# Two mixers of a transformer trunk: a written letter order in place of an emission order from estimates, with TensorE held to it

## The chip, the core and the metric

The kernel runs on one core of a Trainium2 chip. A core has five engines with a queue each: TensorE (PE in the profile; PEld is its weight load), VectorE (DVE), ScalarE (ACT), GpSimd (POOL) and SyncE (SP), which issues the transfers. The metric is the time of one execution in microseconds.

## The reference

A trunk of four residual layers on 512 tokens of width 1024, in FP32. Every layer is half a SwiGLU feed-forward, a mixer, and half a feed-forward again. The mixer of the first layer pair (A) is RWKV-7 time mixing on 12 heads beside a 4-head attention over 256 memory rows; that of the second (B) is dilated sliding-window attention beside the same memory attention. `DEPTH = 2` gives one mixer of each kind, and four feed-forwards.

```python
def step(state, inp):                       # RWKV-7, one token of one head
    r_t, w_t, k_t, v_t, kk_t, a_t = inp
    sa = jnp.einsum('bhvk,bhk->bhv', state, -kk_t)
    state = (state * w_t[:, :, None, :] + sa[..., None] * (kk_t * a_t)[:, :, None, :]
             + v_t[..., None] * k_t[:, :, None, :])
    return state, jnp.einsum('bhvk,bhk->bhv', state, r_t)

logits = jnp.einsum('bshd,bmhd->bhsm', q, k).astype(jnp.float32) / math.sqrt(HEAD_DIM)
probs = jax.nn.softmax(logits, axis=-1)     # memory attention, both mixers
```

## The kernel before

**Products.** All tiles hold features on partitions and the 512 tokens along the free side. A wide FP32 product is made of three matmuls per 128-deep chunk, with both factors split into a high and a low part (`uh`, `ul` against `whi`, `wlo`); those of the mixers' projections show as `mm<-uh,whi`, `mm<-ul,whi`, `mm<-uh,wlo`, and those of the output projections of mixer B as `mm<-kvh,whi` and so on.

**Strands.** The feed-forwards run one after the other. Each mixer is written as a set of generators, the strands, which yield between their steps. In A (`mixer_a`, L654): `finish`, `scan(0)`, `scan(1)`, `prepare`, `memory(0)`, `memory(1)`, `projections`, `first_pass`. In B (`mixer_b`, L1108): `memory`, `dilated(0)`, `dilated(1)`, `settle`, `projections`, `first_pass`. For each of the six head pairs of A, `projections` makes k, r and v; `prepare` makes the decays `E`, the tiles `AR`, `beta`, `kappa`; `scan` (function `rwkv_solve`) multiplies `AR` with `beta` and with `kappa`, masks the first product into `mb` (VectorE), makes `tx` and `TT` from it (GpSimd), transposes in 32x32 blocks (VectorE), and inverts a triangular matrix level by level with small products `sc<-tx,mb` and `sc<-TT,tx`; `finish` carries the state `H` from chunk to chunk (`py<-pt,H` and `py<-H,G`, then ScalarE writes the next `H`) and reads out `y`. `memory` makes logits (`sc<-tmp,memkv`), softmax (VectorE maximum `mx`, ScalarE exponential into `krv` in A or `mpr` in B, VectorE scale), and transposes on TensorE (`sc<-cst,krv`, `sc<-cst,mpr`). `dilated` does the like with `sc<-kh,qn`, `prob`, `dmx`, and `sc<-cst,prob`.

**What sets the order.** `weave` (L312, called at L764 and L1255) picks the next strand to step. Every instruction goes through a helper (`call` in `Engine`, L294, which is therefore the line of all rows below) that adds an estimated cost to a clock per engine in `Meter` (L230). A strand that yields `WAIT` is not stepped until the estimated TensorE clock has reached the estimated end of what it waits for; of those ready the first in the list is taken. `until(test)` holds a strand until other strands have got so far. This gives the order of emission. On top of it the framework's scheduler reorders the instructions of every engine, TensorE too, by its own cost model.

```python
def until(test):
    if not test():
        yield test
```

Of the kernel before, what the change touches and what calls it, by code (L numbers as in the profile page):

```python
# [223 lines left out]
        return r  # L224


WAIT, FREE = "wait", "free"


# [79 lines left out]
            setattr(self, n, Engine(self.meter, n, getattr(nc, n)))  # L309


def weave(meter, strands):  # L312


    live = [[0.0, None, s] for s in strands]
    for x in live:
        x[0] = meter.clock["tensor"]
    while live:
        now = meter.clock["tensor"]
        for x in live:  # L320
            if x[1] and x[1]():
                x[0], x[1] = max(x[0], now), None
        able = [x for x in live if not x[1]]
        assert able, "all strands wait"
        cur = ([x for x in able if x[0] <= now] or [min(able, key=lambda x: x[0])])[0]
        meter.end = max(now, cur[0])
        try:
            said = next(cur[2])
        except StopIteration:
            live.remove(cur)  # L330
            continue
        if callable(said):
            cur[1] = said
        elif said is WAIT:
            cur[0] = meter.end


def until(test):
    if not test():
        yield test  # L340


def run(gen):
    for _ in gen:
        pass


class Net:
# [305 lines left out]
    def mixer_a(self, xin, u, kv, mid, nexts, dst, after):  # L654
        nc, tc = self.nc, self.tc
        w = self.ap["wa_in"]
        with ExitStack() as ctx:
            pool = ctx.enter_context(tc.tile_pool(name="mixa", bufs=1, reuse_waits="tile"))
            pp = ctx.enter_context(tc.tile_pool(name="psa", bufs=2, space=PSUM, reuse_waits="tile"))

            def bank(tag, shape=(P, T)):
                return self.take(pp, list(shape), F32, tag, BANKS[tag])
# [35 lines left out]
            def projections():  # L698
                ps = [bank("mm"), bank("mm")]
                for i, step in enumerate(self.dense([(ps[0], w[0]), (ps[1], w[1])], u.parts, 2)):  # L700
                    if i == 4:
                        rr.append(u.rstd(bank("sc")))
                    yield step
                shifted(ps[0], 0, self.lo)
                nc.scalar.activation(self.lo[:HD], self.lo[:HD], AF.Tanh)
                shifted(ps[1], 1, self.gl)
                nc.scalar.activation(self.gl, self.gl, AF.Tanh, scale=0.5)
                nc.vector.tensor_scalar(self.gl, self.gl, 0.5, 0.5, op0=ALU.mult, op1=ALU.add)
                for j in range(NPAIR):
                    yield from until(lambda: j < 2 or self.made[j - 2])  # L710

                    self.lora[j] = pool.tile([P, 2, P], F32, tag="lora", bufs=3, name=self.nm("lora"))
                    nc.sync.dma_start(self.lora[j][:, 0], self.ap["lo_up"][:, j * P:(j + 1) * P])
                    nc.sync.dma_start(self.lora[j][:, 1], self.ap["g_up"][:, j * P:(j + 1) * P])
                    tiles = []
                    for i in range(3):
                        ps = bank("mm")
                        yield from self.dense([(ps, w[2 + 3 * j + i])], u.parts)
                        t = self.big("krv", 6)
                        shifted(ps, 2 + 3 * j + i, t)  # L720
                        tiles.append(t)
                    self.krv[j] = tiles
                for i in range(2):
                    ps = bank("mm")
                    yield from self.dense([(ps, w[20 + i])], u.parts)
                    nc.vector.tensor_tensor(om[i], ps, rr[0], op=ALU.mult)
                    q.append(om[i])

            def memory(j):
                yield from until(lambda: len(q) > j)  # L730
                r = yield from self.head_rms(q[j], T, self.tmp, bank, keep=self.query_roots[:, j])
                yield from until(lambda: self.made[NPAIR - 1])
                yield from self.memory_attention(j, q[j], r, kv, pool, bank, om[j])

            def spare():
                return tuple(self.xp.tile([P, T], F32R, tag=t, bufs=KD, name=self.nm(t)) for t in ("uh", "ul"))

            def prepare():
                for j in range(NPAIR):
                    yield from until(lambda: self.krv[j] and (j < 2 or len(ys) > j - 2))  # L740
                    yield from self.rwkv_prepare(j)

            def scan(par):
                for j in range(par, NPAIR, 2):
                    yield from until(lambda: self.made[j])
                    yield from self.rwkv_solve(j)

            def finish():
                for j in range(NPAIR):
                    yield from until(lambda: self.made[j])  # L750
                    y = self.big("y", 8)
                    yield from self.rwkv_finish(j, y)
                    ys.append(y)

            def first_pass():
                yield from until(lambda: len(ys) >= NPAIR - 1)
                parts = [spare() for _ in ys[:NPAIR - 1]]
                for p, y in zip(parts, ys):
                    self.split_into(*p, y)
                    yield WAIT  # L760
                yield from self.project_out(xin, parts, 0, "wa_out", bank, [], mid)

            self.busy_vector = True
            weave(self.meter, [finish(), scan(0), scan(1), prepare(), memory(0), memory(1), projections(), first_pass()])  # L764
            pairs = [self.big("AR", 2, (P, 2, T), F32R) for _ in range(2)]
            parts = [(t[:, 0], t[:, 1]) for t in pairs] + [tuple(self.big("krv", 6, dtype=F32R) for _ in range(2))]
            for p, y in zip(parts, (ys[5], om[0], om[1])):
# [340 lines left out]
    def mixer_b(self, xin, u, rkv, ukv, kv, bdram, mid, nexts, dst, after):  # L1108
        nc, tc = self.nc, self.tc
        wq, wkv = self.ap["wb_q"], self.ap["w_kv"]  # L1110
        with ExitStack() as ctx:
            pool = ctx.enter_context(tc.tile_pool(name="mixb", bufs=1, reuse_waits="tile"))
            pp = ctx.enter_context(tc.tile_pool(name="psb", bufs=2, space=PSUM, reuse_waits="tile"))

# [30 lines left out]
            def projections():  # L1145
                for s in range(2):
                    for kind in "qkv":
                        for m in (s, 2 + s, 4 + s):
                            yield from until(lambda: len(later) < 3)
                            yield from project(kind, m)  # L1150
                    if s == 0:
                        for m in (6, 7):
                            yield from project("q", m)

            def settle():
                n = 0
                while n < 20:
                    yield from until(lambda: later)
                    kind, m, t = later.pop(0)
                    n += 1  # L1160
                    if kind == "v":
                        yield WAIT
                        ps = self.turned(lambda b: t[:, b * P:(b + 1) * P])
                        nc.scalar.activation(vt[:, :, m * P:(m + 1) * P], ps, AF.Copy)
                        yield WAIT
                    elif kind == "k":
                        yield from self.head_norm(kh[:, m], t, self.gain(2), self.tmp, bank, T)
                    else:
                        rq[m] = yield from self.head_rms(t, T, self.tmp, bank, keep=self.query_roots[:, m])
                    done.add((kind, m))  # L1170
# [66 lines left out]
            def memory():  # L1237
                for j in range(2):
                    yield from until(lambda: ("q", 6 + j) in done)
                    yield from self.memory_attention(j, q[6 + j], rq[6 + j], kv, pool, bank, om[2 + j])  # L1240
                    remembered.append(j)
# [8 lines left out]
            def first_pass():  # L1250
                yield from until(lambda: len(remembered) == 2 and len(finished) >= 5)
                yield from self.project_out(xin, operands([2, 3]), 0, "wb_out", bank, [], mid)

            self.busy_vector = True
            weave(self.meter, [memory(), dilated(0), dilated(1), settle(), projections(), first_pass()])  # L1255
            run(self.project_out(mid, operands([0, 1]), 2, "wb_out", bank, nexts, dst, ("py", "mm", "sc", "sc"), 3, q))
            self.busy_vector = False
            after()
# [84 lines left out]
```

## Time and profile before

| | us |
|---|---|
| time, median of 3 runs | 2103.12 (2101.11 to 2108.2) |
| profiled execution | 2113.38 |
| its span | 2111.6 |
| mean granted TensorE clock | 0.989 |
| TensorE busy | 2061.6 (98% of the span), 14594 instructions |
| VectorE, ScalarE, GpSimd busy | 867.3, 817.3, 590.7 |

The mixers take the stretches from 386 to 773 us (A) and from about 1541 to 1741 us (B) of the span; what lies outside them is the four feed-forwards. Times within the span are given from its start.

### The profile page before, as it was taken

How to read it: one execution, taken by the hardware profiler on the slowest of the kernel's cores; microseconds unless marked ns; L12 is line 12 of the kernel's file. 1: busy time of each engine (PE TensorE's matmuls, PEld its weight loads, DVE VectorE, ACT ScalarE, POOL GpSimd, SP SyncE). 2: the span in 40 equal slices, each digit the busy share in tenths (PEclk: the TensorE clock that was granted, in tenths of full speed). 3: DMA queues.
4: the chain of work that ended last, by engine and by line, in shares of the span. 5: the costliest groups of instructions: out<-in, count | busy, mean ns of one | idle time of the engine just before them, and what ended most of it. 6: DMA issues, size and time to landing. Idle time of an engine off the chain costs nothing.

```text
span 2111.6 us, 35927 instructions
## 1 busy us (share of the span) xinstructions
PE 2061.6 (98%) x14594; PEld 1670.4 (79%) x14594; DVE 867.3 (41%) x1294; ACT 817.3 (39%) x1418; POOL 590.7 (28%) x513
## 2 busy tenths in 40 slices
PE   8999999989999899999999999999999999999999
PEld 6888888867777677788888888888787768888887
DVE  6333333454555555333343533333326266333322
ACT  6333333423334554333433433333336455333321
POOL 2222222553432152222222222222232224222221
PEclk9999999999999999999999999999999999999999
DMA  5333344411100173353344433334531144333342
GB/s 195 97 95 100 90 127 133 122 47 35 40 29 25 35 244 116 116 166 95 110 138 127 146 99 96 98 103 127 154 95 48 38 156 162 99 96 99 92 138 80
DMA packets 130645, 222.13 MB, mean 105 GB/s; under 512 B 14232, under 2 KB 31824, under 8 KB 130480
## 3 DMA queue, kind: packets, MB, share of 16 engines
q1 hardware_dynamic: 130480, 219.85, 34.0%
q8 instruction: 114, 1.87, 0.4%
q14 instruction: 51, 0.42, 0.1%
HBM read 202.90 MB, written 21.61 MB: 106 GB/s over the span
## 4 chain that ended last, share of the span: by engine, by line
PE 65%; DVE 1%; ACT 0%; issue 0%; POOL 0%; ACTq 0%; POOLq 0%; DVEq 0%
PE fps L294 52%; PE mm L294 7%; PE sc L294 5%; PE py L294 1%; DVE prob L294 0%; DVE x L294 0%; DVE mpr L294 0%; ACT krv L294 0%; DVE mx L294 0%; POOL wlo L294 0%; DVE dmx L294 0%; ACT mpr L294 0%; DVE tmp L294 0%; ACT L294 0%; DVE krv L294 0%
## 5 line engine op out<-in xcount | busy, mean ns | idle before, releaser
L294 POOL TENSOR_TENSOR wlo<-raw,whi 128x512 fp32r<-128x512 f32 (+3 forms) x404 | 496.7, 1231 | 1414.0 <-ACT whi L294 1398.1
L294 ACT ACTIVATE whi<-raw 128x512 fp32r<-128x512 f32 (+3 forms) x684 | 415.7, 610 | 924.4 <-PE fps L294 782.0
L294 PE MATMUL fps<-uh,whi 128*128 128x512 f32 x1408 | 551.8, 392 | 8.2 <-ACT whi L294 8.2
L294 PE MATMUL fps<-uh,wlo 128*128 128x512 f32 x1408 | 550.5, 391 | 0.6 <-POOL wlo L294 0.6
L294 PE MATMUL fps<-ul,whi 128*128 128x512 f32 x1408 | 549.1, 390 | 0.0
L294 DVE TENSOR_TENSOR wlo<-raw,whi 128x512 fp32r<-128x512 f32 x280 | 201.7, 721 | 343.7 <-ACT whi L294 338.7
L294 PEld LDWEIGHTS fps<-uh,whi 128*128 128x128 f32 x1408 | 264.9, 188 | 68.7 <-ACT whi L294 12.9
L294 PEld LDWEIGHTS fps<-uh,wlo 128*128 128x128 f32 x1408 | 265.2, 188 | 58.6 <-POOL wlo L294 3.1
L294 PEld LDWEIGHTS fps<-ul,whi 128*128 128x128 f32 x1408 | 265.0, 188 | 55.8 <-issue 0.7
L294 PE MATMUL fps<-hh,whi 128*128 128x512 f32 x704 | 273.9, 389 | 0.0
L294 PE MATMUL fps<-hl,whi 128*128 128x512 f32 x704 | 273.9, 389 | 0.0
L294 PE MATMUL fps<-hh,wlo 128*128 128x512 f32 x704 | 273.9, 389 | 0.0
L294 DVE TENSOR_TENSOR gs<-fps,rstd 128x512 f32<-128x512 f32 x88 | 60.5, 690 | 321.6 <-PE fps L294 321.6
L294 PEld LDWEIGHTS fps<-hh,whi 128*128 128x128 f32 x704 | 132.2, 188 | 27.7
L294 PEld LDWEIGHTS fps<-hh,wlo 128*128 128x128 f32 x704 | 132.2, 188 | 27.3
L294 PEld LDWEIGHTS fps<-hl,whi 128*128 128x128 f32 x704 | 132.2, 188 | 27.3
L294 PE MATMUL mm<-uh,whi 128*128 128x512 f32 x280 | 124.6, 445 | 0.4 <-DVE p L294 0.2
L294 PE MATMUL mm<-ul,whi 128*128 128x512 f32 x280 | 114.5, 409 | 0.1
L294 PE MATMUL mm<-uh,wlo 128*128 128x512 f32 x280 | 113.6, 406 | 0.0
L294 DVE TENSOR_TENSOR hm<-fps,gs 128x512 f32<-128x512 f32 x88 | 60.6, 691 | 121.9 <-PE fps L294 115.7
L294 DVE TENSOR_TENSOR hl<-hm,hh 128x512 fp32r<-128x512 f32 x88 | 77.2, 880 | 50.7 <-ACT hh L294 50.7
L294 PEld LDWEIGHTS mm<-uh,whi 128*128 128x128 f32 x280 | 54.1, 193 | 16.2 <-issue 4.4
(260 smaller groups left out, 2049.6 us busy)
## 6 DMA issues: line engine op xcount, KB each, us to landing
raw<-w SPq DMA_DIRECT2D x512, 256.0 KB, 2.7
raw<-wa_in SPq DMA_DIRECT2D x44, 256.0 KB, 2.8
xd<-x SPq DMA_DIRECT2D x40, 256.0 KB, 2.7
tmp<-xd SPq DMA_DIRECT2D x32, 256.0 KB, 4.2
xin<-xd SPq DMA_DIRECT2D x32, 256.0 KB, 4.3
raw<-w_kv SPq DMA_DIRECT2D x24, 256.0 KB, 2.7
raw<-w SPq DMA_DIRECT2D x32, 128.0 KB, 2.4
raw<-wmem SPq DMA_DIRECT2D x16, 256.0 KB, 2.6
```

The lines of the kernel that those rows point to most:

```text
L294: r = f(*args, **kw)
```

## The change

`weave` gets a string for each mixer. Each letter stands for one step of one strand (`a` is the first in the list, `b` the second, and so on). A letter whose strand still waits in `until` is owed and taken as soon as its test holds. `until` now always yields once. The `Meter`'s estimates are no longer asked. In both mixers a manual schedule is set for TensorE, so that its instructions keep the order in which they are emitted. The other engines are still ordered by the framework's scheduler, now from another order of emission.

```diff
+ORDER_A = (
+    "abcdeaefhhhhhhggggggggfgggggggggggggggggggggggggggggggggggggdddgddggggddddddggdgggggddbbbbbbbggggggb"
...
+ORDER_B = (
+    "ccccabdedfeeeeeeeeeeeeeeeeeeeddddeeddddeeeeeeeeeddddeebbeeebbeeeedaadeedeeddeeeeeddeeeedddeeeeeeedde"
...
-def weave(meter, strands):
...
-        cur = ([x for x in able if x[0] <= now] or [min(able, key=lambda x: x[0])])[0]
-        meter.end = max(now, cur[0])
...
+def weave(strands, order):
+    tests, owed = {}, []
+
+    def step(k):
+        if k in tests and not tests[k]():
+            return False
+        tests.pop(k, None)
+        said = next(strands[k], None)
+        if callable(said):
+            tests[k] = said
+        return True
+
+    for letter in order:
+        owed.append(ord(letter) - 97)
+        while True:
+            k = next((k for k in dict.fromkeys(owed) if step(k)), None)
+            if k is None:
+                break
+            owed.remove(k)
+    assert not owed, "a strand still waits"
+    for s in strands:
+        assert next(s, None) is None, "the order ends early"
 
 def until(test):
-    if not test():
-        yield test
+    yield test
...
+            ctx.enter_context(tc.manual_schedule(engines={mybir.EngineType.PE}))
...
-            weave(self.meter, [finish(), scan(0), scan(1), prepare(), memory(0), memory(1), projections(), first_pass()])
+            weave([finish(), scan(0), scan(1), prepare(), memory(0), memory(1), projections(), first_pass()], ORDER_A)
...
+            ctx.enter_context(tc.manual_schedule(engines={mybir.EngineType.PE}))
...
-            weave(self.meter, [memory(), dilated(0), dilated(1), settle(), projections(), first_pass()])
+            weave([memory(), dilated(0), dilated(1), settle(), projections(), first_pass()], ORDER_B)
```

The set of instructions is the same: both kernels issue the same 11341 TensorE products in the program, and as many ScalarE table loads (41). Outside the two mixers TensorE's order is the same. Within them it changes at 399 places from one strand to another before and at 367 now, and between tile sizes (full 128x128 products, and products packed into parts of the array) 225 times before and 221 now in A, 44 and 37 in B. Line 294 of the helper becomes line 309. In the rows below, numbers behind a tile's name tell buffers apart; they are not the same in the two kernels.

**First place: TensorE in mixer A, the solve of the third head pair,** from the last of its products with `kappa` on. `mb` is made from the products with `beta` that stand ahead of these. Before:

```order
L294 MATMUL sc_5158<-AR_4915,kappa_4996 64x128
L294 MATMUL py_5045<-pt_5039,H_5107 64x64 x2
L294 MATMUL py_5046<-H_5107,G_5040 64x64 x2
L294 MATMUL sc_5188<-cst,beta_4950 128x128 x4
L294 MATMUL sc_5196<-cst,kappa_4996 128x128 x4
L294 MATMUL mm_4965<-uh_2651,whi_5207 128x512
L294 MATMUL mm_4965<-ul_2652,whi_5207 128x512
L294 MATMUL mm_4965<-uh_2651,wlo_5208 128x512
L294 MATMUL py_5046<-pt_5039,H_5107 64x64 x2
L294 MATMUL py_5045<-H_5107,G_5040 64x64 x2
L294 MATMUL sc_5218<-tx_5203,mb_5149 32x32 x32
```

Now:

```order
L309 MATMUL sc_5055<-AR_4927,kappa_4936 64x128
L309 MATMUL mm_4908<-uh_2883,whi_4991 128x512
L309 MATMUL mm_4908<-ul_2884,whi_4991 128x512
L309 MATMUL mm_4908<-uh_2883,wlo_4992 128x512
L309 MATMUL sc_5078<-mb_4364,WU_5005 64x64 x2
L309 MATMUL sc_5079<-mb_4364,WU_5005 64x64 x2
```

Here the pair of `AR` products has moved ahead of the readouts of an earlier pair's `finish` (the rows with `WU`), and 133 matmuls (15 full ones, 8 of 128x128 and 110 of 64x64) stand between the last `kappa` product and the first `tx,mb` product, where 19 stood.

**Second place: VectorE in mixer A, the first solve, at the last level of its inversion.** `TT<-TT,sc` and the transpose into `tx` behind it are links of the solve; `krv<-tmp,vec,p` is a token shift of a later projection. Before:

```order
L294 TENSOR_TENSOR p_4058<-mm_3769,rstd_3243 128x512
L294 SCALAR_TENSOR_TENSOR tmp_3867<-krv_3515,kks_3202,sc_4010 128x512
L294 SCALAR_TENSOR_TENSOR tmp_4055<-tmp_3823,tmp_3867 128x512
L294 TENSOR_TENSOR TT_3649<-TT_3649,sc_4016 128x256
L294 SCALAR_TENSOR_TENSOR krv_4057<-tmp_4061,vec,p_4058 128x512
L294 STREAM_TRANSPOSE tx_4074<-TT_3649 128x256
```

Now:

```order
L309 TENSOR_TENSOR p_3981<-mm_3824,rstd_3245 128x512
L309 SCALAR_TENSOR_TENSOR krv_3980<-tmp_3984,vec,p_3981 128x512
L309 SCALAR_TENSOR_TENSOR tmp_3779<-krv_3529,kks_3204,sc_3997 128x512
L309 TENSOR_TENSOR tx_4044<-sc_4011,cst 128x256
L309 SCALAR_TENSOR_TENSOR tmp_4005<-tmp_3777,tmp_3779 128x512
L309 SCALAR_TENSOR_TENSOR beta_4007<-tmp_4005,tmp_3891 128x512
L309 TENSOR_SCALAR tmp_3777<-tmp_3777,ka_3206,ka_3208 128x512
L309 TENSOR_TENSOR TT_3625<-TT_3625,sc_4056 128x256
L309 TENSOR_TENSOR tmp_3777<-krv_3529,tmp_3777 128x512
L309 STREAM_TRANSPOSE tx_4090<-TT_3625 128x256
```

The token shift has moved ahead of the two links, and a plain multiply stands between them instead.

**Third place: TensorE in mixer B, near its end, from the last dilated logits to the transposes of their probabilities.** Before, the rows ahead of the transposes are (the `mm` rows are the first pass of the output projection):

```order
L294 MATMUL mm_16326<-kvh_16235,whi_16330 128x512
L294 MATMUL mm_16326<-kvl_16236,whi_16330 128x512
L294 MATMUL mm_16326<-kvh_16235,wlo_16331 128x512
L294 MATMUL mm_16326<-kvh_16239,whi_16330 128x512
L294 MATMUL mm_16326<-kvl_16240,whi_16330 128x512
L294 MATMUL mm_16326<-kvh_16239,wlo_16331 128x512
L294 MATMUL mm_16327<-kvh_16235,whi_16365 128x512
L294 MATMUL mm_16327<-kvl_16236,whi_16365 128x512
L294 MATMUL sc_16167<-cst,prob_16114 128x128 x4
```

Now:

```order
L309 MATMUL sc_16121<-kh,qn_14703 128x512
L309 MATMUL sc_16126<-kh,qn_14705 128x128
L309 MATMUL sc_16127<-kh,qn_14705 128x128
L309 MATMUL sc_16126<-kh,qn_14707 128x128
L309 MATMUL sc_16127<-kh,qn_14707 128x128
L309 MATMUL sc_16146<-kh,qn_14703 128x512
L309 MATMUL sc_16147<-kh,qn_14703 128x512
L309 MATMUL sc_16152<-kh,qn_14705 128x128
L309 MATMUL sc_16153<-kh,qn_14705 128x128
L309 MATMUL sc_16152<-kh,qn_14707 128x128
L309 MATMUL sc_16153<-kh,qn_14707 128x128
L309 MATMUL sc_16172<-cst,prob_16119 128x128 x4
```

The sixteen `mm` products that stood between the logits and the transposes (the last eight of them are shown) have moved behind them.

## Rows read from the trace of the kernel before

**Rows 1.** The page's list of engines: busy time, share of the span, instructions.

```profile
PE 2061.6 (98%) x14594; PEld 1670.4 (79%) x14594; DVE 867.3 (41%) x1294; ACT 817.3 (39%) x1418; POOL 590.7 (28%) x513
```

**Rows 2.** Busy time of each engine by stretch; the columns are the stretch, its length, then each engine's busy time, and at the end the granted TensorE clock (PEclk), the share of the DMA engines and GB/s. The stretches are mixer A, the two feed-forwards between the mixers, and mixer B.

```profile
386.00:773.00 387.00, 358.60 (x6756) 276.34 (x6755) 194.74 (x347) 159.06 (x306) 148.35 (x156) 0.96 0.19 58
773.00:1541.00 768.00, 766.56 (x3414) 630.38 (x3413) 302.17 (x393) 284.88 (x467) 196.67 (x157) 1.00 0.41 125
1541.00:1741.00 200.00, 193.06 (x1134) 150.28 (x1133) 90.67 (x185) 100.84 (x202) 52.50 (x47) 0.97 0.25 79
```

**Rows 3.** TensorE's waits in mixer A (386 to 773 us): waiting operation, what ended the wait; us in total, times, longest.

```profile
PE sc L294 <- DVE tx L294: 14.0, 11, 3.0
```

**Rows 4.** TensorE's waits in mixer B (1541 to 1741 us), in the same columns.

```profile
PE mm L294 <- DVE x L294: 3.8, 2, 3.6
PE sc L294 <- DVE mpr L294: 1.7, 2, 0.9
```

**Rows 5.** The timeline in mixer A at the solve of the third pair: start, duration, engine, operation, count, and in brackets the engine's idle time ahead of it with what ended it.

```profile
536.47 0.39 PE L294 MATMUL mm<-ul,whi 128*128 128x512 f32 x1
536.71 0.40 PE L294 MATMUL mm<-uh,wlo 128*128 128x512 f32 x1
537.03 0.27 PE L294 MATMUL py<-pt,H 64*64 64x64 f32 x2
...
537.20 1.05 PE L294 MATMUL sc<-AR,beta 64*64 64x128 f32 x32
538.32 1.29 DVE L294 TENSOR_TENSOR mb<-sc,cst 128x512 f32<-128x512 f32 x2 [2.81 <-PE py L294]
539.69 1.29 POOL L294 TENSOR_TENSOR tx<-mb,cst 128x512 f32<-128x512 f32 x1 [0.74 <-DVE mb L294]
541.05 0.72 POOL L294 TENSOR_TENSOR TT<-tx 128x256 f32<-128x256 f32 x1
...
541.12 0.23 PE L294 MATMUL py<-H,G 64*64 64x64 f32 x2
541.41 0.32 ACT L294 ACTIVATE H<-py,E 128x64 f32<-128x64 f32 x1 [0.35 <-PE py L294]
541.86 0.72 POOL L294 TENSOR_TENSOR TT<-TT,cst 128x256 f32<-128x256 f32 x1
542.61 0.45 DVE L294 STREAM_TRANSPOSE tx<-TT 128x256 f32<-128x256 f32 x1 [1.81 <-POOL E L294]
543.20 0.75 PE L294 MATMUL sc<-tx,mb 32*32 32x32 f32 x64 [1.86 <-DVE tx L294]
...
544.48 0.63 PE L294 MATMUL mm<-ul,whi 128*128 128x512 f32 x1
544.90 0.63 PE L294 MATMUL mm<-uh,wlo 128*128 128x512 f32 x1
```

**Rows 6.** TensorE's timeline at five other waits in mixer A: the same product in the solves of the first, fourth and fifth pair, a product later in the first solve, and the sums of the first pair.

```profile
433.81 1.35 PE L294 MATMUL sc<-tmp,cst 128*128 128x512 f32 x2 [1.92 <-DVE tmp L294]
...
443.87 0.74 PE L294 MATMUL sc<-tx,mb 32*32 32x32 f32 x64 [1.54 <-DVE tx L294]
...
451.77 0.41 PE L294 MATMUL sc<-TT,tx 32*32 32x32 f32 x27 [1.57 <-DVE tx L294]
...
592.25 0.73 PE L294 MATMUL sc<-tx,mb 32*32 32x32 f32 x63 [1.86 <-DVE tx L294]
...
641.01 0.74 PE L294 MATMUL sc<-tx,mb 32*32 32x32 f32 x64 [1.85 <-DVE tx L294]
```

**Rows 7.** The timeline at the last level of the first solve.

```profile
464.22 0.41 DVE L294 TENSOR_TENSOR TT<-TT,sc 128x256 f32<-128x256 f32 x1
...
466.39 1.73 DVE L294 SCALAR_TENSOR_TENSOR krv<-tmp,vec,p 128x512 f32<-128x512 f32 x1 [1.76 <-POOL tmp L294]
468.05 0.43 DVE L294 STREAM_TRANSPOSE tx<-TT 128x256 f32<-128x256 f32 x1
...
468.62 1.02 PE L294 MATMUL sc<-tx,mb 32*32 32x32 f32 x32 [2.96 <-DVE tx L294]
```

**Rows 8.** Four short stretches behind waits of TensorE, in the columns of rows 2; the third column from the end is the granted clock.

```profile
468.00:476.00 8.00, 7.38 (x79) 5.73 (x79) 4.76 (x8) 1.38 (x3) 3.05 (x3) 0.57 0.10 35
543.50:547.50 4.00, 4.00 (x128) 2.98 (x115) 0.70 (x2) 1.29 (x3) 0.00 (x0) 0.57 0.02 4
642.50:650.00 7.50, 6.95 (x90) 5.70 (x89) 1.56 (x3) 1.92 (x4) 1.85 (x2) 0.54 0.01 2
1649.00:1657.00 8.00, 6.27 (x24) 3.34 (x23) 3.35 (x5) 3.39 (x9) 2.67 (x2) 0.79 0.22 66
```

**Rows 9.** The timeline of a memory attention in mixer A, from the maximum of its logits to the transposes.

```profile
713.96 0.68 DVE L294 TENSOR_REDUCE mx<-sc 128x2 f32<-128x512 f32 x1
...
721.22 1.29 PE L294 MATMUL sc<-cst,krv 128*128 128x128 f32 x5 [2.06 <-DVE krv L294]
```

**Rows 10.** The timeline in mixer B at the last dilated logits of the third place.

```profile
1697.53 2.40 PE L294 MATMUL sc<-kh,qn 64*128 64x512 f32 x12 [0.39 <-DVE prob L294]
...
1701.43 3.40 DVE L294 TENSOR_REDUCE dmx<-prob 128x2 f32<-128x1536 f32 x2
...
1705.56 0.79 PE L294 MATMUL mm<-kvh,whi 128*128 128x512 f32 x1 [3.59 <-DVE x L294]
...
1709.14 2.47 PE L294 MATMUL sc<-cst,prob 128*128 128x128 f32 x12
```

More of the change, by code (lines that the diff above doesn't have):

```diff
@@ L224, in rstd @@
         return r
+ORDER_A = (
+    "abcdeaefhhhhhhggggggggfgggggggggggggggggggggggggggggggggggggdddgddggggddddddggdgggggddbbbbbbbggggggb"
+    "ddggbbggdbgggggbbgdbdgbbggddddbddggbbggggbggbbgeeeegbdgbbddgaacccaaccaaccgaagaagaacggagaccaaagggaacg"
+    "gacchhhhgaaaagcddgdhhhhgccgggcdccdggcggddddddbbccgcggaaaaadcgddgcaggagaaagabbbbbgaaabgaaabbggaabgabg"
+    "ggbgagaaabdbddbgggbgbbddbggddddddbgbbggbbgaadaagaagddgaacaaccaagaagcaaaccggggccaccgacaccggaaaagggcdd"
+    "dccgcgccddbbgggcgdddddddccgcggccdgaadaagaagbaabaabbbaagaabgaaabbgaabaggbgggbgagaaagbdddbbgggbdccgbbg"
+    "dgbddddddbffcfbbdbbaaddaaaaaacaacccecaaffaacceaaacfcecceeccfaaffecccaeceafaaaacffcchchcahaahaaaahaaa"
+    "haaahaaahhaahhaahaahhhhhhhhhhhhhhhhhhhhh"
+)
+ORDER_B = (
+    "ccccabdedfeeeeeeeeeeeeeeeeeeeddddeeddddeeeeeeeeeddddeebbeeebbeeeedaadeedeeddeeeeeddeeeedddeeeeeeedde"
+    "edddeeeedeeeeddeeeeedddeeeeeeeedddecceebeeeeeeeeeeeeebddddbbbbbbbceccccccceeeadeedddeffffeeebaaabbee"
+    "eeeeeeeacaaaadddcceeeeaedaaeeaeeeedddeeeeeaeaaeddddedddeeedddeeeeeededeedddeeeeeeddeedddbbbbeeeecccc"
+    "eedddeeeeeeeeeeeeeeeebdddddcbbbbffccfbbbbcfcccfccffbbffbffcffcc"
+)
 WAIT, FREE = "wait", "free"
@@ L309, in __init__ @@
             setattr(self, n, Engine(self.meter, n, getattr(nc, n)))
-def weave(meter, strands):
[L315 to L324, printed above, removed]
-        cur = ([x for x in able if x[0] <= now] or [min(able, key=lambda x: x[0])])[0]
-        meter.end = max(now, cur[0])
[L327 to L331, printed above, removed]
-        if callable(said):
-            cur[1] = said
-        elif said is WAIT:
-            cur[0] = meter.end
+def weave(strands, order):
[5 more added lines that the diff above has]
+        said = next(strands[k], None)
+        if callable(said):
+            tests[k] = said
[10 more added lines that the diff above has]
+        assert next(s, None) is None, "the order ends early"
 def until(test):
-    if not test():
-        yield test
+    yield test
 def run(gen):
```

## The prediction, written before the result was known

> **What bounds the kernel now.** I read the list of engines first, then the table by stretch, then TensorE's waits in the two mixers, then short timelines at the longest waits, and last the order of each engine before and now. TensorE is busy for 2061.6 of 2111.6 us; no other engine reaches half of that [rows 1]. The feed-forwards leave almost nothing: 766.56 of 768 us between the mixers, at full clock [rows 2]. What a change of order can touch is in the mixers: 387 − 358.6 = 28.4 us without TensorE work in A and 200 − 193.1 = 6.9 us in B. There is a second loss: the granted clock is 0.96 in A and 0.97 in B [rows 2]. At half clock (1.2 of 2.4 GHz) a stretch does half the work, so its loss is 387 × 0.04 ≈ 15.5 us in A and 200 × 0.03 ≈ 6 us in B (the two means are rounded, hence ±2 and ±1). All of it together is 28.4 + 6.9 + 15.5 + 6 ≈ 57 us; that is the ceiling of any gain, as the products are the same.
>
> Half of A's idle time has one name. TensorE waits 14.0 us in 11 pieces for `tx`, the transposed tile of the solve [rows 3]. In B two waits stand out: 3.6 us for `x`, and 1.7 us in two pieces for `mpr` [rows 4].
>
> **Part 1, the head of each solve (first place).** The chain is: product `AR,beta`, mask on VectorE (1.29 us for two), three steps on GpSimd (1.29, 0.72, 0.72), a transpose on VectorE (0.45), product `tx,mb` [rows 5]. The first product starts at 537.20 and lasts 1.05, so the chain runs from 538.25 to 543.20: 4.95 us, of which TensorE waited 1.86 and worked 3.09. The same wait stands in three more solves, at 1.54, 1.86 and 1.85 us [rows 6]. The four make 7.1 us. Now the pair of products has moved ahead of a `finish`'s readouts. At the place shown, 15 full matmuls stand in the gap, which start 0.23 to 0.24 us apart [rows 5], so 3.5 us; and the `kappa` product, as long as that with `beta` (1.05 us for 32, or 0.033 each), and 110 small ones at about that price give 1.05 + 3.6. That is 8.1 us without the eight others, against 4.95 needed. The other three gaps, counted the same way, hold 5.4 us or more. I take all four waits as gone: **−7.1** (bounds: 0 if the other engines come late to it by what TensorE gains, −7.1).
>
> **Part 2, the levels of the inversion (second place).** At the last level of the first solve a token shift on VectorE (1.73 us) stands between the sum into `TT` and its transpose, and TensorE waits 2.96 [rows 7]. Now a 0.69 us multiply is there instead, about 1 us less; and the work under the gap, counted as above, grows from 2.4 to 3.1 us: 1.7 us gained together. The wait of 1.57 us one level up [rows 6] has 3.6 us of work in its place now and goes too. In two later solves the shift also moves behind the transpose, but the work under them shrinks by as much; I give them nothing. **−3.3** (bounds 0 and −4.5, both waits whole).
>
> **Part 3, the clock behind those waits.** Behind them the granted clock is 0.57 for 8 us, 0.57 for 4 us and 0.54 for 7.5 us, where it is 1.00 in the feed-forwards [rows 8, 2]; full matmuls start 0.42 us apart instead of 0.24 [rows 5]. What it costs is 0.43 × 8 + 0.43 × 4 + 0.46 × 7.5 = 8.6 us. If the clock fell because of these waits, it goes with them; but each has shorter ones near it that stay. I take somewhat over half, **−5** (bounds 0 and −8.6).
>
> **Part 4, mixer B.** The two waits for `mpr` (1.7 us) get 7.3 us of work over them where 6.0 stood: −1.7. The clock there is 0.79 for 8 us [rows 8], which is 8 × 0.21 = 1.7 us; −1.7. At the third place the work is taken away: the softmax from the last logits' end (1697.53 + 2.40 = 1699.93) to the transposes at 1709.14 takes 9.2 us, in which the first pass ran, with a wait of 3.59 us for its bank, as VectorE was in the two reductions (3.40 us) [rows 10]. Now the second logit group's own 2.2 us or so are all that stands under it. The rest, 9.2 − 2.2 ≈ 7.0, is waited for; the 3.59 us are saved: +3.4 (bounds: 0 if the scheduler lets the reductions start sooner, +5.6 if both logit groups come before). Sum for B **0** (−3.4 to +2).
>
> **Part 5, what the fixed order uncovers in A.** Behind a state product ScalarE needs until 541.41 + 0.32 = 541.73 from 541.12, 0.61 us, for the next `H` [rows 5]. Before, other products stood in almost every such gap, and I saw no wait for `H` above 0.2 us. Now six gaps, in the last two pairs' `finish`, hold none: 6 × 0.65 = **+3.9** (bounds 0, +5). The memory attention's softmax needs, from its first maximum at 713.96 to the transposes at 721.22, 7.3 us with a table load in it, or some 5.5 by the sum of its parts [rows 9]. In two places it now has 3.3 and 3.9 us of work under it: 2.2 + 1.6 = 3.8 of waiting. Before, it cost one wait of 2.06 [rows 9]: net **+1.7** (bounds −1, +4.5). The sums of the first pair, which wait 1.92 now [rows 6], have less work ahead: **+0.9** (0, +2).
>
> **Part 6, turns between tile sizes.** A full matmul starts 0.24 us behind another (536.47 to 536.71), but a packed one 0.32 behind a full one [rows 5]: 0.08 us. Eleven fewer turns in A and B together give **−1** (0, −1; the way out of a packed one is not larger). The Trainium skill (TensorEngine Tiling (Array Packing), Key Properties) says that a change of tiling mode drains TensorE; the 0.08 us agree in sign, and the page gives no price.
>
> The strand switches fall too (399 to 367), but a switch without a turn has no price in any row; nothing. The other engines' instructions are the same ones, under a TensorE that is busy 98%; nothing, beyond the places above. The transfers on SP are the same, and I found no place where a weight is loaded later than its matmul needs.
>
> **Sum.** −7.1 − 3.3 − 5 + 0 + 3.9 + 1.7 + 0.9 − 1 = −9.9 us, on the profiled execution's 2113.38: 2103.5, a ratio of 0.9953. On the median of 2103.12, which lies 0.5% below the profiled one, this is **2093 us**. The bounds of the terms, all at once, give −26 to +14; they will not all fall to one side.
>
> **The rivals.**
>
> *A: the gain is larger.* The parts above are counted at the waits that I looked at. If the new order also takes most of the small ones and TensorE keeps its clock, the ceiling of 57 us counts. Two fifths to two thirds of it would be −23 to −38, thus 2065 to 2080 us. For it: most of A's half clock stands near waits that go. Against: A's new order makes holes of its own (part 5).
>
> *B: nothing.* The chain of a solve is serial over three engines. A wait removed at its head lets TensorE arrive earlier at the next link, and if the chain bounds the stretch, the wait turns up there (the 14.0 us are 11 pieces [rows 3], so there are next links). Then ±6 us: 2097 to 2109. Against: TensorE has 358.6 us of work in the 387 us, so the chains have room in most of A.
>
> *C: slower.* TensorE kept to a written order must stand at any operand that is late, with all its later products queued behind it, though others are ready. Part 5's short hops at their upper bounds (+5, +4.5, +2), part 4's softmax at +5.6, and 2 us lost to a half clock behind each of the three new waits of 2 us or more would be +23 against the −16.4 of parts 1 to 3 and 6: +7, thus 2110. It decides from where the new waits' sum passes some 17 us. The Trainium skill (TensorE: Matmul & The Clock Gate, Part 3, "The mechanism") says that matmuls start and end in program order, with no reordering, so a late one holds all. The trace agrees: 1.86 us of nothing at 543.20 with full matmuls ready behind.
>
> *D: the change does not do what it says.* TensorE's order has changed (first place), so this is out.
>
> **How the numbers follow.** Chances: the forecast, −4 to −20 us around its sum, 0.45; A 0.20; B 0.22; C 0.13. 0.3% is about what a measurement of this kernel can tell from no change: 2096.8 to 2109.4. Of the forecast's 0.45 I put 0.05 above 2096.8. Faster: 0.40 + 0.20 = 0.60; same: 0.05 + 0.22 = 0.27; slower: 0.13. The range from 2070 to 2108 leaves out about 0.08 of A below and 0.12 of C above. The forecast's own range is 2083 to 2099.
>
> **What would show it.** Right: TensorE waits for `tx` in A fall from 14.0 to about 4 us, the waits for `H` rise to about 4; A's stretch is shorter by 8 to 14 us and its mean clock 0.97 or more; B's is within 3 us of before, with one wait of about 7 us at its end; the feed-forwards take the same time. It would be wrong if the waits for `tx` are as long as before under other levels (B), if the granted clock falls at the six `H` gaps, or if VectorE or GpSimd take the solve's steps later than TensorE's order supposes (C).

## The result, and the profile after

The changed kernel takes 2097.4 us (median of 10 runs, 2095.2 to 2099.6). The kernel before, run 10 times beside it, takes 2109.0 (2101.1 to 2113.2). The ratio is 0.995, with an interval of 0.9935 to 0.9964: half a per cent faster, as the predicted ratio of 0.9953 said. The predicted 2093 us was that ratio on the median of three early runs, which lay 6 us under the later median.

The two profiled executions lie further apart than the medians: 16.7 us by their spans, against 11.6. The one of the kernel before took 2113.4 us, 4.4 more than its median, and the one of the changed kernel 0.7 less than its own. A difference between two stretches below is therefore good to a few us only.

The stretches, cut exactly where TensorE's first and last product of each mixer stand; first the kernel before (A, then B), columns as in rows 2. The windows of rows 2 were rougher: B begins at 1521 us and not at 1541.

```profile
386.44:764.57 378.13, 349.73 (x6718) 269.19 (x6717) 190.09 (x340) 153.22 (x295) 141.85 (x149) 0.96 0.17 53
1520.76:1735.03 214.27, 206.12 (x1196) 160.64 (x1195) 94.99 (x189) 104.72 (x207) 57.86 (x49) 0.98 0.29 88
```

The changed kernel (A, then B):

```profile
385.36:752.25 366.89, 346.04 (x6718) 266.85 (x6717) 183.50 (x340) 153.22 (x295) 141.27 (x149) 0.97 0.17 54
1507.91:1717.06 209.15, 198.80 (x1196) 159.43 (x1194) 97.90 (x190) 104.60 (x206) 58.69 (x50) 0.98 0.28 89
```

A is 11.2 us shorter, B 5.1. In A TensorE's idle time falls from 28.4 to 20.9 us. The rest of A's gain is busy time, 3.7 us, with the same products. TensorE's waits in A before, behind the 14.0 us for `tx` [rows 3] ("issue" is time in which the engine waited for nothing that the profile shows):

```profile
PE sc L294 <- issue: 3.2, 6, 0.8
PE py L294 <- issue: 2.9, 3, 1.3
PE sc L294 <- DVE krv L294: 2.1, 1, 2.1
...
PE sc L294 <- ACT krv L294: 1.8, 1, 1.8
PE sc L294 <- ACT tmp L294: 1.1, 3, 0.6
...
PE py L294 <- ACT H L294: 0.2, 1, 0.2
```

And now:

```profile
PE sc L309 <- ACT tmp L309: 3.5, 4, 1.2
PE py L309 <- ACT H L309: 3.2, 5, 1.5
PE sc L309 <- DVE tx L309: 3.0, 6, 0.8
PE sc L309 <- DVE tmp L309: 1.8, 1, 1.8
PE sc L309 <- issue: 1.7, 2, 1.1
PE py L309 <- DVE G L309: 1.5, 1, 1.5
PE py L309 <- issue: 1.4, 2, 0.8
PE sc L309 <- DVE krv L309: 1.3, 2, 1.0
PE sc L309 <- DVE mb L309: 1.2, 1, 1.2
```

And in B now:

```profile
PE sc L309 <- DVE prob L309: 7.8, 4, 6.2
...
PE sc L309 <- DVE mpr L309: 0.9, 1, 0.9
```

The 14.0 us for `tx` [rows 3] are 3.0. The 3.2 us for `H` are new but for 0.2, as are 1.5 us for `G`, 1.2 for `mb` and 2.4 of the 3.5 for ScalarE's `tmp`. In B the 3.6 us for `x` [rows 4] are gone, and one wait of 6.2 us for `prob` stands at the third place.

### The profile page after: what moved, and what is told of

It is laid out like the page before. It is cut to its first block, busy times and chain, and to the rows that moved or that the text cites. A ratio compares the mean times of both kernels' runs of the same rounds, so it can differ in the third digit from the quotient of the medians.

```text
span 2094.9 us, 35917 instructions
## 1 busy us (share of the span) xinstructions
PE 2049.4 (98%) x14594; PEld 1666.8 (80%) x14594; DVE 860.6 (41%) x1294; ACT 817.0 (39%) x1418; POOL 588.4 (28%) x513
## 4 chain that ended last, share of the span: by engine, by line
PE 71%; DVE 2%; ACT 1%; issue 0%; DMA 0%; ACTq 0%; DVEq 0%
PE fps L309 52%; PE mm L309 10%; PE sc L309 8%; PE py L309 2%; ACT krv L309 0%; DVE prob L309 0%; DVE x L309 0%; DVE mx L309 0%; DVE dmx L309 0%; DVE ul L309 0%; DVE mpr L309 0%; ACT L309 0%; DVE tx L309 0%; ACT tmp L309 0%; DMA xd<-x 0%
```

## The experiments

All ratios are against the kernel before, run on the same chip in the same series. There are four series, each on another chip: `e1` to `e4`, `e5` to `e8`, `e9` to `e11`, and `e12`. Times from different series are best compared by these ratios.

**Where the gain is: one mixer at a time.** `e1_only_a` has the letters and the held order in A only, `e2_only_b` in B only; the other mixer has the old `weave`, and TensorE free. Of the edit of `e1_only_a`:

```diff
-            ctx.enter_context(tc.manual_schedule(engines={mybir.EngineType.PE}))
...
-            weave([memory(), dilated(0), ... first_pass()], ORDER_B)
+            weave_old(self.meter, [memory(), dilated(0), ... first_pass()])
```

> Mixer A follows its letters and TensorE keeps them there; mixer B is as before. If the gain is the sum of places (theory), this is A's share of it: the two profiles give 11.3 us of 16.7 in A, so of the measured 0.995 a ratio near 0.9966 (range 0.995 to 0.998), the waits for tx in A near 3 us and those for H near 3 us, B's stretch at 214 us as before. Rival: A's new waits eat up its gain, and the gain came from B and from the spread of the kernel before: 0.999 to 1.001.

Measured: 0.9948 (0.9931 to 0.9964), 2098.2 us.

> Mixer B follows its letters and TensorE keeps them there; mixer A is as before. Theory by the two profiles: 5.1 of 16.7 us, a ratio near 0.9984 (range 0.997 to 1.000), B's stretch near 209 us with one wait of about 6 us at its end. By the prediction's own sum for B: 1.000. Rival (B carries the gain): 0.996 or less.

Measured: 0.9975 (0.9963 to 0.9987), 2104.5 us. A alone gives all that the change gives; B alone gives a quarter of a per cent, which isn't seen on top of A. Those two don't add, and the intervals are too wide to say why.

**The two edits apart.** `e3_tables_free` keeps the letters and drops both lines that hold TensorE. `e4_hold_only` keeps those lines and goes back to the old `weave`.

```diff
-            ctx.enter_context(tc.manual_schedule(engines={mybir.EngineType.PE}))
```

> Both mixers follow the letters, but the scheduler may move TensorE's instructions, as before. It moves about a third of A's and a sixth of B's products away from the written order. If the order itself is what matters and TensorE must keep it (theory), about half of the gain is lost: 0.997 to 0.999, waits for tx in A between 3 and 14 us. Rival 1, the emission order does it all: 0.995. Rival 2, the scheduler's liberty was a help and the written order pays too many short hops: 0.993 or less, with fewer waits for H.

Measured: 0.9886 (0.9869 to 0.9902), 2085.9 us. The second rival was right: without the hold it is 12 us faster than the changed kernel.

> The order of emission is that of the estimates, as before, but TensorE keeps it in both mixers. If the tables are what matters (theory): no gain, 1.000 to 1.005, since a late operand holds all behind it; waits for tx 14 us or more. Rival, the scheduler's moves on TensorE were the fault and not the estimates: 0.995 to 0.997, with the waits for tx falling as they do after the change.

Measured: 1.0216 (1.0199 to 1.0234), 2155.2 us. So the letters alone, with the scheduler free, are worth 24 us, and holding TensorE costs: 45 us on the old order, 12 on the letters. The stretches of `e4_hold_only`, A and B, show it in the idle time (37.5 and 27.8 us) and in the clock:

```profile
385.68:777.79 392.11, 354.57 (x6718) 275.04 (x6717) 190.32 (x340) 153.79 (x295) 141.49 (x149) 0.93 0.17 51
1533.45:1766.21 232.76, 204.93 (x1196) 160.44 (x1195) 94.29 (x190) 106.06 (x207) 57.33 (x49) 0.96 0.24 75
```

**Which mixer's hold costs.** `e5_again` is the changed kernel, `e6_hold_a` holds TensorE in A only, `e7_hold_b` in B only; the letters stay.

> The changed kernel itself, as the measure for the others of this call: 0.995 (0.993 to 0.997), 2096 to 2100 us.

Measured: 0.9944, 2097.7 us.

> Both tables; TensorE keeps its order in mixer A alone, and in B the scheduler may move it. Without any hold the tables gave 0.9886. If the price of holding lies in A (theory, by the stages of the two profiles: A 366.9 us held and 355.0 free; B with the feed-forward behind it 581.9 held and 582.6 free): like the changed kernel, 0.994 to 0.996. Rival, B's wait of 6 us is the price: 0.991 to 0.993.

Measured: 0.9947 (0.9932 to 0.9962), 2098.6 us.

> Both tables; TensorE keeps its order in mixer B alone, and in A the scheduler may move it. Theory (the price lies in A): like the tables without any hold, 0.988 to 0.9895, A's stretch near 355 us. Rival (B): 0.992 to 0.994.

Measured: 0.9888 (0.9871 to 0.9905), 2085.7 us. The price is A's, as far as ratios with intervals of ±0.0015 can tell. The stretch A of `e7_hold_b`, and its waits there:

```profile
385.84:738.70 352.86, 339.69 (x6718) 259.76 (x6717) 186.10 (x340) 152.04 (x295) 140.68 (x149) 1.00 0.19 57
```

```profile
PE sc L309 <- DVE tmp L309: 4.7, 3, 3.6
PE sc L309 <- DVE tx L309: 2.7, 4, 1.2
...
PE py L309 <- ACT H L309: 0.9, 1, 0.9
```

Against `e5_again` of the same series (its stretch A stands under part 3 below) A is 11.1 us shorter. Of that 9.1 are idle time, 13.2 us against 22.3; the granted clock is 1.00 against 0.98. Of the waits for `H` 0.9 us stay, and those for `G`, `mb` and ScalarE's `tmp` are gone, while those for VectorE's `tmp` grew from 1.8 to 4.7. What the scheduler did can be read where the held order waits 1.45 us for `G` (part 1 below): it put full products ahead of the state product, and 0.80 us of waiting are left.

```profile
530.19 0.40 PE L309 MATMUL mm<-ul,whi 128*128 128x512 f32 x1
531.38 0.33 PE L309 MATMUL py<-H,G 64*64 64x64 f32 x4 [0.80 <-ACT whi L309]
```

In its order the tile size changes 243 times in A; in the held letters 221 times, and in the slowest kernel, `e4_hold_only`, 201 times.

**Part 1 undone.** `e8_heads_back` puts the `AR` products of three solves (third, fourth, fifth pair) back behind the readouts and the first state products. Letters moved in the third pair, `b` being its solve (moved to behind the sixth state product):

```diff
-...bb g c aaaaaa gg a g aa a g a bbb bb g...
+...   g c aaaaaa gg a g aa a g a bbbbb bb g...
```

> The changed kernel with part 1 undone in three solves (third, fourth and fifth pair): the AR products stand again behind the readouts of finish and the first state products, with some 3 to 3.4 us of TensorE work between the first product's end and the tx,mb product, where 4.95 is needed. Theory (part 1 as predicted): three waits for tx of 1.5 to 1.9 us come back, about +5 us, and up to +9 if the clock falls behind them: 2102 to 2107 us when the changed kernel takes 2098. Rival: the early products make VectorE's masks stand ahead of the pt and G of finish (TensorE waits 1.5 us for G there now) and the clock falls there instead, so that undoing gives back as much as it takes: within 2 us of the changed kernel, or faster.

Measured: 0.9981 (0.9968 to 0.9994), 2105.2 us: 7.5 us more than `e5_again`. Its waits in A, and the heads of the three solves:

```profile
PE sc L309 <- DVE tx L309: 7.1, 8, 1.9
PE py L309 <- ACT H L309: 5.4, 10, 1.5
...
PE sc L309 <- DVE mb L309: 2.4, 2, 1.2
...
PE sc L309 <- DVE mk L309: 1.5, 1, 1.5
```

```profile
537.28 0.74 PE L309 MATMUL sc<-tx,mb 32*32 32x32 f32 x64 [1.90 <-DVE tx L309]
...
589.41 0.75 PE L309 MATMUL sc<-tx,mb 32*32 32x32 f32 x64 [1.50 <-DVE mk L309]
...
639.08 0.74 PE L309 MATMUL sc<-tx,mb 32*32 32x32 f32 x64 [1.91 <-DVE tx L309]
```

All three head waits are back in their places: 1.90, 1.50 and 1.91 us where before had 1.86, 1.86 and 1.85 [rows 5, 6]. The profile puts the second down to `mk`, so it isn't among those for `tx`. The rival has one point: the 1.5 us for `G` are gone here, so the early products did cause them; they are the smaller part.

**Gaps filled by hand, with TensorE held.** `e9_tail_fill` moves twelve first-pass products ahead of the transposes at B's third place. `e10_hops_filled` puts a step into each of six gaps of `finish`. `e12_lifted` lifts eight steps of A's first pass into the gaps behind the last projection, splitting its operands earlier.

Parts of the three edits (the letters change with them in `e9_tail_fill` and `e12_lifted` too):

```diff
# e9
-                yield from until(lambda: len(remembered) == 2 and len(finished) >= 5)
+                yield from until(lambda: len(remembered) == 2 and len(finished) >= 4)
# e10, the last finish
-haahaaaahaaahaaahaaahhaa
+haahaahaahaahahaaahaaahh
# e12
-                yield from until(lambda: len(ys) >= NPAIR - 1)
+                yield from until(lambda: len(ys) >= NPAIR - 2)
```

> The changed kernel with twelve first-pass products of mixer B moved ahead of the transposes at the third place (the first pass is let go one unit earlier for it). Theory (part 4: what stands under the softmax decides): the wait of 6.2 us for prob falls by four steps of 0.69 us to about 3.4, and the time by 2.5 to 3 us, to some 2095 us when the changed kernel takes 2097.7. Rival (as in the kernel before): the first pass's banks are emptied by VectorE behind its two reductions, and a wait for x takes the place: within 1 us of the changed kernel.

Measured: 2096.2 us (2093.2 to 2100.3), 0.994 (0.992 to 0.996). The wait fell by 1.8 us, not 2.8:

```profile
PE sc L309 <- DVE prob L309: 6.0, 4, 4.4
```

The time is 1.5 us less than that of `e5_again`, which ran in another series, and inside the scatter of the runs: not settled.

> The changed kernel with a full or transposing step put into six of the gaps of part 5 (between a state product and the next one that needs its H): two projections in the third pair's finish, the two transposes of beta and kappa in the fifth's, two first-pass steps in the last one's. Theory (0.65 us apiece, as predicted; the first gap waits 1.5 us for G): 3 to 4 us less, 2094 us when the changed kernel takes 2097.7, and less again where the clock no longer falls at 530 and 677 us. Rival: the added turns (0.1 us each) and the steps missing later take it back: within 1 us.

Measured: 2099.7 us, 0.9955 (0.9938 to 0.9972); no gain. Its waits in A:

```profile
PE sc L309 <- ACT tmp L309: 5.4, 6, 1.5
PE sc L309 <- issue: 3.5, 5, 1.4
...
PE py L309 <- ACT H L309: 1.9, 2, 1.5
```

The waits for `H` fell by 1.3 us and that for `G` went (1.5); those for `tmp` and at issue grew by 1.9 and 1.8. The gaps went to the next link.

> The changed kernel, TensorE held in both mixers, with eight steps (24 full products) of mixer A's first pass lifted by hand into the gaps near its end, as the scheduler does it when it may: its first four operands are split as soon as four outputs are there, and its first two outputs are worked side by side. In the changed kernel TensorE waits there for mb (1.2 us), H (1.5 and 0.7), krv (1.3) and two levels of the last solve (1.5). Theory (the hold costs 12 us in A because ready products can't be pulled into gaps, most of it behind the last projection): 4 to 6 us less, 2092 to 2094 us when the changed kernel takes 2097.7. Rival (as with the six filled hops): the gaps move to the next link, and the time stays within 1.5 us of the changed kernel.

Measured: 2098.7 us, 0.9951 (0.9935 to 0.9968); no gain. TensorE now waits for an operand of the lifted products:

```profile
PE mm L309 <- ACT uh L309: 1.3, 1, 1.3
```

The waits for `H` fell by 1.9 us and those for `mb` by 0.9; the 1.3 for `uh` are new, and those at issue grew.

So filling a few gaps by hand doesn't bring back what the scheduler's liberty brings. That it lies in many small moves all through A is what remains; it wasn't shown place by place.

**Both gains together.** `e11_best` holds TensorE in B only and has the twelve products in front.

> Both tables, TensorE held in mixer B alone, with the twelve first-pass products in front as above. If the two effects add (2085.7 us with the hold in B alone, less 2.5 to 3): 2083 us, a ratio of 0.987 to 0.988. If the wait only moves: 2086.

Measured: 2084.7 us (2082.1 to 2086.7), 0.9886 (0.9864 to 0.9909). It doesn't differ from `e3_tables_free` and `e7_hold_b`. These three beat both kernels; the simplest is the changed one without its two `manual_schedule` lines.

## Why the prediction was right, point by point

**Part 1 (−7.1) held.** The four waits at the head of the solves went; three of the four products now start without a wait like this, and the fourth at 540.72 below:

```profile
441.57 0.75 PE L309 MATMUL sc<-tx,mb 32*32 32x32 f32 x64
...
588.39 0.75 PE L309 MATMUL sc<-tx,mb 32*32 32x32 f32 x64
...
632.15 0.75 PE L309 MATMUL sc<-tx,mb 32*32 32x32 f32 x64
```

Undoing three of them cost 7.5 us, of which 5.3 are the waits themselves, for 5.6 in the prediction. The work that it counted under the gap of the third solve, 8.1 us, was too little: the trace has two records for each of the small products (32 of `AR,beta`, where the program has 16), so 110 of them cost twice what it gave them. That only makes its conclusion safer. It left out the head of the last solve, which waited 1.8 us for ScalarE's `krv` before and waits no more. And it missed a cost: VectorE's masks of the early products stand ahead of `pt` and `G` of the running `finish`. In the changed kernel, third pair:

```profile
529.21 0.60 DVE L309 TENSOR_TENSOR G<-sc,cst 128x192 f32<-128x192 f32 x2
529.96 0.33 PE L309 MATMUL py<-H,G 64*64 64x64 f32 x4 [1.45 <-DVE G L309]
...
540.72 0.77 PE L309 MATMUL sc<-tx,mb 32*32 32x32 f32 x58
```

The `tx,mb` product at 540.72 waits for nothing, but TensorE stood 1.45 us at 529.96.

**Part 2 (−3.3) held.** The last level of the first solve waits 0.41 us where it waited 2.96 [rows 7], and the wait of 1.57 [rows 6] is one of 0.79 at another level:

```profile
461.05 0.75 PE L309 MATMUL sc<-TT,tx 32*32 32x32 f32 x64 [0.79 <-DVE tx L309]
...
465.16 0.69 PE L309 MATMUL sc<-tx,mb 32*32 32x32 f32 x32 [0.41 <-DVE tx L309]
```

**Part 3 (−5): right in kind, and not a fixed size.** The half clock left the first two places of rows 8 and the one in B; at the fifth solve 3.4 us of it remain where there were 6.8. It came up at others. In the changed kernel, behind the 1.45 us above:

```profile
530.60:540.80 10.20, 10.11 (x66) 6.53 (x70) 1.45 (x2) 3.12 (x8) 2.37 (x3) 0.51 0.10 27
```

`e5_again`, the same program, has the same wait (1.47 us), and the clock behind it stays up. It ran A in 363.95 us at a mean clock of 0.98 in place of 366.89 at 0.97:

```profile
531.20:541.40 10.20, 9.79 (x208) 6.93 (x209) 2.74 (x5) 5.31 (x13) 3.77 (x5) 1.00 0.11 29
385.26:749.21 363.95, 341.67 (x6718) 263.77 (x6717) 183.57 (x340) 152.98 (x295) 141.44 (x149) 0.98 0.18 54
```

Its busy time is 4.4 us less and its idle time 1.4 more. So 3 us of A differ from one execution to the next, and the half clock is what differs: in all A has 30.7 us of it before, 23.9 in the changed kernel and 13.7 in `e5_again`. One sign that the prediction gave for being wrong did come: in both executions the clock fell at gaps of a late `finish` that wait for `H`. In the changed kernel:

```profile
677.50:684.30 6.80, 5.57 (x108) 4.22 (x110) 3.27 (x9) 3.08 (x9) 0.92 (x2) 0.50 0.00 0
678.29 0.37 PE L309 MATMUL py<-pt,H 64*64 64x64 f32 x2 [1.49 <-ACT H L309]
```

**Part 4 (0) was the term that failed in size: B's stretch became 5.1 us shorter**, less 1.3 that the feed-forward behind it lost (376.6 to 377.8 us to the end). The tail's wait came as worked out (6.2 against 7.0 us, and 3.6 saved), and of the two waits for `mpr` one went and one stayed. B's idle time rose by 2.2 us in all; the gain is busy time, 206.1 to 198.8 us. A part of what the sum missed stood in the trace of before, behind the wait of 3.59 us [rows 10], a stretch at half clock full of first-pass products:

```profile
1705.00:1712.00 7.00, 6.44 (x23) 5.23 (x23) 4.39 (x10) 5.25 (x11) 0.00 (x0) 0.56 0.70 214
```

It cost some 7 × 0.44 = 3.1 us (an estimate). In the profile of the changed kernel the half clock falls into the wait itself, where it costs little (TensorE is busy for 3.29 of 6.8 us):

```profile
1684.30:1691.10 6.80, 3.29 (x18) 2.99 (x20) 5.11 (x11) 5.20 (x11) 0.00 (x0) 0.51 0.00 0
1687.81 2.79 PE L309 MATMUL sc<-cst,prob 128*128 128x128 f32 x12 [6.17 <-DVE prob L309]
```

That isn't all of it. With B's old order in `e1_only_a` and the new one in `e7_hold_b` the mean clock is the same, and B is still 3.4 us shorter and TensorE's busy time 5.6 us less:

```profile
1505.23:1718.42 213.19, 205.05 (x1196) 160.03 (x1195) 95.00 (x189) 104.75 (x207) 57.78 (x49) 0.98 0.29 88
1494.74:1704.54 209.80, 199.44 (x1196) 160.25 (x1194) 97.87 (x190) 104.59 (x206) 58.67 (x50) 0.98 0.29 89
```

Which property of the new order makes the same products shorter there isn't shown.

**Part 5 (+6.5) came out near its size, but by other waits than it named: that was luck.** Of its three places the waits for `H` rose by 3.0 us (3.9 forecast), the memory attention's for `krv` fell from 2.1 to 1.3 (+1.7 forecast), and the first pair's went from 1.9 to 1.8 (+0.9 forecast): +2.1 together. Not seen ahead were `G` (1.5), `mb` (1.2) and ScalarE's `tmp` (+2.4), 5.1 together; against that, the waits at issue fell by 3.0, and some small ones came. All but the solves' waits rose by some 5 us. The mechanism, a TensorE that stands at a late operand though other products could run, is what taking the hold away shows.

**Part 6 (−1) can't be seen:** the kernels stand in time against their number of turns, from 243 (fast) to 201 (slow), so anything that the turns cost is hidden by larger effects.

**The sum.** By the two profiles A's waits at the solves fell by 12.8 us (11.0 for `tx` and the 1.8 at the last head; parts 1 and 2 say 10.4), the others rose by 5 (part 5 says 6.5), and busy time fell by 3.7 (part 3 says 5, and part 6 has its share). So A came out by its mechanism, 11.2 us for a forecast of some 9. B gave 3.8 that the sum didn't have, and the profiles together show 5 us more than the medians do. That −9.9 met the measured −11.6 so closely is in part luck.

The 24 us of the letters and the 12 us of the hold are another split, which the sum doesn't make: they are measured against a TensorE that the scheduler orders. The sum sets the changed kernel against the one before, and has no term for what the letters do with the scheduler free.

**The rivals.** Rival A's 23 to 38 us were to be had, at their lower end, but by the letters without the hold. Rival C named the hold's mechanism, and it does decide on the old order (2155 us). That the change would be better without its hold was in no case of the prediction.

## What to carry to other kernels

Where a change does two things, price each alone: here one is worth 24 us and the other costs 12. In this kernel the best was to give the scheduler a better order to start from and leave it free; whether holding pays elsewhere, a run has to show. In a serial chain move the product that feeds the slow engines early, and look at what these then do later; gaps that were merely filled opened again one link on, in two tries of three.

## What the runs showed of the hardware that was not expected

The same program differs by 12 us from run to run before the change (2101 to 2113), and the time follows the granted clock: in the series of `e9` to `e11` the kernel before ran from 2099.6 us at a mean clock of 0.996 to 2116.5 at 0.987. With the scheduler free in A the clock is 0.995 to 0.998, and the runs differ by 0.7 us (`e3_tables_free`, four runs), 3.7 (`e7_hold_b`, five) and 4.6 (`e11_best`, six). Fewer waits needn't be the reason: `e4_hold_only`, which waits most, lies within 2.9 us in its four runs, all near 0.98.

The same wait of about 1.5 us, at the same place of the same program, had 10.2 us at half clock behind it in one execution and none in another (part 3).
